# Forgetting attention begun by halves of the tokens, its value weights kept on chip, later sums in the post norms

## The chip, the cores and the metric

One core of a Trainium2 chip runs the whole program. Its engines work at the same time, each through an instruction queue of its own: TensorE (PE) multiplies, VectorE (DVE), ScalarE (ACT) and GpSimd (POOL) do elementwise work, and SyncE (SP) issues the transfers. The metric is the device time of one execution in microseconds (us), lower is better.

## What is computed

512 tokens of width 1024 go through two blocks. Block one is a mixer (gated linear attention, sliding-window attention and pooling, merged by gates, projected by `w_out`) and a conv-GeGLU feed-forward layer; both end in a norm of the result before it is added to x. Block two has forgetting attention ("fox"), a feed-forward layer, latent attention, another feed-forward layer and a last norm. The change touches the seam from the mixer's output to the first feed-forward layer, and the seam from there to fox:

```python
        x = x + rmsnorm(merged @ w_out[l], norm_mix_post[l])
        h = rmsnorm(x, norm_ffn_pre[l])
        f = conv_ffn(h, ffn_w_up[l], ffn_conv_w[l], ffn_conv_b[l], ffn_w_down[l])
        x = x + rmsnorm(f, norm_ffn_post[l])
...
    proj = h @ w_in
    qkv = proj[..., :3 * FOX_WIDTH].reshape(b, s_len, 3, FOX_HEADS, FOX_HEAD_DIM)
    q, k, v = qkv[:, :, 0], qkv[:, :, 1], qkv[:, :, 2]
    logf = jax.nn.log_sigmoid((proj[..., 3 * FOX_WIDTH:] + b_f).astype(jnp.float32))
    cum = jnp.cumsum(logf, axis=1)
```

## The kernel before

Activations lie with the channels on the partitions, x as eight tiles of 128 x 512 (tokens along the row). A product in fp32 accuracy is three matmuls: each operand is split into a rounded high part and a low rest, and high x high, high x low and low x high are added in PSUM. Weights come from memory in chunks of 128 x 1024 (512 KB, eight units of 128 x 128) in the order of a plan (`tfk_plan`). `_split` (lines 266 to 282) sends one chunk into a `raw` buffer (there are two), ScalarE casts it to `hi` (L277), VectorE subtracts to get `lo` (L278). The next-but-one transfer waits until both have read `raw`. `hi` and `lo` come from a pool of three buffers each; where `tfk_kept` holds for all units of a chunk (weights that are used twice) they are `khi` and `klo` in slots, large buffers shared with activations, and stay there until their second use.

A sublayer's end is `post_norm` (from L936). Its last projection tiles are done by halves of the tokens (256 each), so that the second half is computed while the first is finished. Each half's `chain(h)` is: sums of squares over the channels by TensorE (tile `tok`, two columns per half), a reciprocal square root in small steps on VectorE (`ra`, `ry`, `rh`, `rt`, L470 to L481), a diagonal matrix of it (`diag`, L490), which a matmul with ones spreads over all partitions (`bc`); then for each of eight tiles VectorE scales `yo` by `bc` (L962), GpSimd adds it to x (L963), and `x_ready` (L533) makes what the next sublayer needs: high part of x times the gain on ScalarE (`xs`, L420), low part on VectorE (`xs`, L421), squares on ScalarE (`sq`, L504), added up in `acc` by GpSimd, the eighth tile's by VectorE (L507). After the second half, one task (`stats`) takes the sums of all four token groups (`tok`, four columns), the square root, and `bc` of 512 columns, copied to `rsb`: the norm factor that the next sublayer multiplies into its results, not into its inputs, so its matmuls can begin before the factor is there.

The order of TensorE's work is written by the program: a clock counts the matmuls issued, and a task such as a chain's sums or its `bc` is put in when the clock has passed its due time, a number in `LAG`. The order on the other engines comes from a scheduler when the program is built, with no regard to the chip's real times: what stands in an engine's queue is done in that order, and an instruction whose input is late holds up all behind it.

Around the two places, in before: after `wout` come 288 matmuls of `up0` (six tiles, two halves of 256 tokens, 144 each, weights in `khi`, `klo`), whose results stay in PSUM until `rsb` is there. After `down0` comes `fox`: values for heads 0 to 7 of the first half (`fv`, 48 matmuls of 512 columns), the forget gates (`narrow`, 16), the first query tile (`fq`, 24), then the same for the second half with `fv`'s weights sent again, then the values of heads 8 to 15 for all tokens (96 matmuls), then keys (`fk`) and scores. Values are split into `fV` with the norm factor of their tokens.

## Time and profile before

| | |
|---|---|
| median of 3 runs (lowest, highest) | 2225.93 us (2223.95, 2228.35) |
| the profiled execution | 2225.05 us |
| its span in the profile | 2223.3 us |
| busy: PE, DVE, ACT, POOL | 97%, 64%, 46%, 13% |
| chain that ended last: PE, DVE, ACT, issue | 84%, 9%, 3%, 2% |
| chunk transfers (raw), median time to landing | 359 of 512 KB, 3.5 us |

The profile is one execution on the chip. A timeline row gives start and duration of an instruction, or of several alike in a row, and in brackets how long the engine stood idle before it and what ended that. Matmul durations overlap; the distance between starts is their pace. PEclk in the windows is the granted clock of TensorE as a share of full speed; 1.00 is 2.4 GHz, the lower of its two levels, 1.2 GHz, is 0.5.

### The profile page before, as it was taken

The page shows a single profiled execution, that of the slowest core. Times are in us where ns is not written, and L with a number is a line of the kernel's source. Part 1 is how long each engine was busy: PE and PEld are TensorE (multiplying, and loading weights), DVE is VectorE, ACT ScalarE, POOL GpSimd, SP SyncE. Part 2 cuts the span into 40 slices and gives each one's busy share as a digit, 9 for nine tenths or more (in the row PEclk, how much of TensorE's full clock was granted, in tenths as well). Part 3 has the DMA queues.
Part 4 walks back from the last instruction along what each step waited for, and adds up shares of the span by engine and source line. Part 5 has one row for each costly group of instructions (what it writes and reads, how often), then busy time and mean ns, then how long its engine had stood idle before and what let it go on. Part 6 is the DMA issues. An engine that isn't in the chain of part 4 may idle for free.

```text
span 2223.3 us, 27520 instructions
## 1 busy us (share of the span) xinstructions
PE 2165.1 (97%) x10536; PEld 1822.0 (82%) x10536; DVE 1423.7 (64%) x2372; ACT 1022.2 (46%) x1676; POOL 282.1 (13%) x242
## 2 busy tenths in 40 slices
PE   8989999999999998999999999999999999999998
PEld 6777788898888897888888888887888888888887
DVE  6897545578777238787677774357646567777524
ACT  4454232445444235676544443245755655444322
POOL 5221000040000004464200000102100101000010
PEclk9999999999999999999999999999999999999999
DMA  4211333322233344433233323332122223333332
GB/s 163 76 39 48 95 95 95 114 89 73 96 101 97 95 126 133 134 105 97 84 93 97 95 95 98 101 100 76 48 76 67 67 60 98 99 95 95 96 103 96
DMA packets 61956, 206.29 MB, mean 93 GB/s; under 512 B 7152, under 2 KB 9584, under 8 KB 61824
## 3 DMA queue, kind: packets, MB, share of 16 engines
q1 hardware_dynamic: 61392, 203.74, 29.4%
q8 instruction: 83, 1.36, 0.2%
q10 hardware_dynamic: 432, 0.79, 0.1%
q14 instruction: 49, 0.40, 0.1%
HBM read 197.65 MB, written 2.13 MB: 90 GB/s over the span
## 4 chain that ended last, share of the span: by engine, by line
PE 84%; DVE 9%; ACT 3%; issue 2%; DMA 1%; POOL 0%; SPq 0%; DVEq 0%; ACTq 0%; POOLq 0%
PE up L340 32%; PE down L340 15%; PE mout L340 4%; PE uq L340 3%; PE sc L340 2%; PE gate_a L340 2%; PE gate_b L340 2%; PE gate_c L340 2%; PE wout L340 2%; PE fout L340 2%; DVE lo L278 2%; DVE xs L421 1%; PE mpo L340 1%; PE dq L340 1%; PE fq L340 1%
## 5 line engine op out<-in xcount | busy, mean ns | idle before, releaser
L278 DVE TENSOR_TENSOR lo<-raw,hi 128x1024 fp32r<-128x1024 f32 (+1 forms) x348 | 438.1, 1259 | 318.0 <-ACT hi L277 313.6
L340 PE MATMUL up<-xs,hi 128*128 128x512 f32 x2016 | 621.8, 390 | 0.0
L277 ACT CAST hi<-raw 128x1024 fp32r<-128x1024 f32 (+1 forms) x348 | 365.2, 1049 | 554.2 <-PE down L340 170.5
L340 PEld LDWEIGHTS up<-xs,hi 128*128 128x128 f32 x2016 | 378.3, 188 | 78.9 <-issue 1.0
L340 PE MATMUL up<-xs,lo 128*128 128x512 f32 x1008 | 392.2, 389 | 0.0
L340 PE MATMUL down<-hl,hi 128*128 128x512 f32 (+1 forms) x1188 | 332.6, 366 | 0.0
L340 PEld LDWEIGHTS down<-hl,hi 128*128 128x128 f32 x1188 | 214.9, 189 | 36.2
L340 PEld LDWEIGHTS up<-xs,lo 128*128 128x128 f32 x1008 | 189.3, 188 | 39.6
L340 PE MATMUL down<-hl,lo 128*128 128x512 f32 (+1 forms) x594 | 217.1, 365 | 0.0
L507 POOL TENSOR_TENSOR acc<-acc,sq 128x256 f32<-128x256 f32 (+1 forms) x48 | 56.1, 1169 | 765.2 <-ACT sq L504 763.6
L1024 DVE TENSOR_TENSOR u<-up,rsb 128x512 f32<-128x512 f32 x132 | 90.1, 685 | 80.9 <-PE up L340 76.7
L1026 ACT ACTIVATE c<-u,par 128x512 f32<-128x512 f32 x132 | 107.0, 814 | 59.9 <-DVE u L1024 59.8
L340 PEld LDWEIGHTS down<-hl,lo 128*128 128x128 f32 x594 | 112.0, 189 | 18.0
L1027 DVE SCALAR_TENSOR_TENSOR c<-u,par,c 128x511 f32<-128x511 f32 x132 | 98.3, 746 | 23.8 <-ACT c L1026 23.7
L963 POOL TENSOR_TENSOR x<-x,yo 128x256 f32<-128x256 f32 x32 | 28.6, 930 | 633.3 <-DVE yo L962 633.3
L1028 DVE SCALAR_TENSOR_TENSOR c<-u,par,c 128x510 f32<-128x510 f32 x132 | 98.8, 749 | 4.0
L340 PE MATMUL uq<-hl,hi 128*128 128x512 f32 x288 | 89.5, 391 | 1.4 <-POOL hl L458 1.4
L457 ACT CAST hl<-c 128x512 fp32r<-128x512 f32 x66 | 40.7, 617 | 104.6 <-DVE c L1035 104.6
L340 PE MATMUL mout<-hl,hi 128*128 128x512 f32 x256 | 79.9, 393 | 0.0
L1033 ACT ACTIVATE c<-c 128x512 f32<-128x512 f32 x66 | 41.6, 630 | 70.4 <-DVE c L1028 70.3
L421 DVE SCALAR_TENSOR_TENSOR xs<-x,par,xs 128x512 fp32r<-128x512 f32 (+1 forms) x64 | 61.9, 1005 | 8.0 <-ACT xs L420 8.0
L340 PEld LDWEIGHTS uq<-hl,hi 128*128 128x128 f32 x288 | 53.9, 188 | 13.3 <-POOL hl L458 1.8
(398 smaller groups left out, 3933.9 us busy)
## 6 DMA issues: line engine op xcount, KB each, us to landing
raw<-in_wall_dram SPq DMA_DIRECT2D x359, 512.0 KB, 3.5
K<-KH SPq DMA_DIRECT2D x36, 128.0 KB, 2.3
bias<-cumd SPq DMA_DIRECT2D x16, 256.0 KB, 4.1
out_dram<-x SPq DMA_DIRECT2D x8, 256.0 KB, 2.3
x<-in_x_dram SPq DMA_DIRECT2D x7, 256.0 KB, 6.0
raw<-in_wall_dram SPq DMA_DIRECT2D x2, 256.0 KB, 3.9
early<-in_cst_dram SPq DMA_DIRECT2D x1, 512.0 KB, 6.5
msk<-in_msk_dram SPq DMA_DIRECT2D x1, 512.0 KB, 6.6
```

The source lines that it names most:

```text
L277: nc.scalar.copy(out=hi[:, c], in_=raw[:, c])
L278: nc.vector.tensor_tensor(out=lo[:, c], in0=raw[:, c], in1=hi[:, c].bitcast(F32), op=ALU.subtract)
L340: self.nc.tensor.matmul(out, lhsT=a, rhs=b, start=start, stop=stop)
L421: nc.vector.scalar_tensor_tensor(out=lo, in0=src, scalar=scale, in1=hi.bitcast(F32), op0=ALU.mult, op1=ALU.subtract)
L457: nc.scalar.copy(out=hi, in_=src)
L507: (eng or self.nc.vector).tensor_tensor(out=acc[:, cols], in0=acc[:, cols], in1=sq[:, cols], op=ALU.add)
L963: nc.gpsimd.tensor_tensor(out=x, in0=x, in1=yt, op=ALU.add)
L1024: v.tensor_tensor(out=u, in0=ps, in1=rsb, op=ALU.mult)
L1026: nc.scalar.activation(out=c, in_=u, func=AF.Identity, scale=self.p(conv, 88 + t), bias=self.p(conv, 132 + t))
L1027: v.scalar_tensor_tensor(out=c[:, 1:], in0=u[:, 0:T - 1], scalar=self.p(conv, 44 + t), in1=c[:, 1:], op0=ALU.mult, op1=ALU.add)
L1028: v.scalar_tensor_tensor(out=c[:, 2:], in0=u[:, 0:T - 2], scalar=self.p(conv, t), in1=c[:, 2:], op0=ALU.mult, op1=ALU.add)
L1033: nc.scalar.activation(out=g, in_=g, func=func)
```

## The change

1. The plan sends `fv`'s first half once (4 chunks fewer: 355 in the place of 359), in chunks of its own (`align`), and `tfk_kept` holds for `fv`, so all its chunks are `khi`, `klo` in slots.
2. The second chain's sums are due later: `keep_up` 6.5 after `wout`, `keep_fv` 9.0 after `down0`, in the place of 3.5.
3. The next sublayer's norm factor comes by halves (`half_stats_task`): two columns of sums, a root and a `bc` of 256 columns for each half.
4. `fox` does the values by halves: heads 0 to 7 and 8 to 15 of the first half, then both of the second.
5. Two masks (`lows`) move from a constant buffer into slots (39 in the place of 37), filled with zeros by GpSimd where they are needed.

```diff
@@ -112,6 +112,5 @@
     ffn(0)
+    align()
     cols("fv", 0, 8, 0, 4)
-    align()
     cols("fq", 0, 8, 0)
-    cols("fv", 0, 8, 0, 4)
     cols("fv", 0, 8, 4, 4)
@@ -158,3 +157,3 @@
     return e and (e[0] == "wout" and e[2] >= WOUT_WHOLE or e[0] == "up0" and (e[2] % DFF_T) * 2 < UP0_FIRST
-                  or e[0] == "fq" and e[2] == 0)
+                  or e[0] == "fq" and e[2] == 0 or e[0] == "fv")
 
@@ -167,3 +166,3 @@
 LAG = {
-    "sums_first": 19.0, "lat": 3.19, "lat_rsqrt": 5.85, "sums": 8.32, "sums_late": 13.0, "rsqrt": 6.9, "chain": 5.9, "keep": 3.5,
+    "sums_first": 19.0, "lat": 3.19, "lat_rsqrt": 5.85, "sums": 8.32, "sums_late": 13.0, "rsqrt": 6.9, "chain": 5.9, "keep": 3.5, "keep_up": 6.5, "keep_fv": 9.0,
     "last": 2.8, "last_rsqrt": 3.7,
@@ -205,3 +204,3 @@
         self.psum = ctx.enter_context(tc.tile_pool(name="psum", bufs=8, space=bass.MemoryType.PSUM))
-        self.nslot, self.nt2 = 37, 9
+        self.nslot, self.nt2 = 39, 9
         self.x = [self.slot([P, 2, T], F32, "x") for _ in range(4)]
@@ -214,3 +213,2 @@
         nc.gpsimd.memset(self.ones, 1.0)
-        self.lows = [self.cpool.tile([P, 2, T], F32R, name=f"lows{i}") for i in range(2)]
         self.ident = self.c("ident", 128)
@@ -432,2 +430,8 @@
 
+    def make_lows(self, n):
+        self.lows = [self.slot([P, 2, T], F32R, "lows") for _ in range(n)]
+        for a in self.lows:
+            for j in range(2):
+                self.nc.gpsimd.memset(a[64 - 64 * j:128 - 64 * j, j].bitcast(F32), 0.0)
+
     def stack_k(self, k):
@@ -525,2 +529,16 @@
 
+    def half_stats_task(self, acc, h):
+
+        pt = self.ps("tok")
+        self.tok_sums(acc, pt, (2 * h, 2 * h + 1))
+        rs = self.rsqrt(pt[:, 0:2], 1.0 / 1024, 2)
+        yield LAG["rsqrt"]
+        pb = self.bcast(rs)
+        if h == 0:
+            self.rsb = self.pool.tile([P, T], F32, tag="rsb", name="rsb", bufs=2)
+        self.nc.scalar.copy(out=self.rsb[:, HALVES[h]], in_=pb[:, 0:256])
+        self.rs_half[h].set(rs)
+        if h == 1:
+            self.rs.set((self.rsb, None))
+
     def x_start(self, nxt):
@@ -532,2 +550,3 @@
             self.xs = [Fut(self) for _ in range(8)]
+            self.rs, self.rs_half = Fut(self), [Fut(self) for _ in range(2)]
 
@@ -556,4 +575,6 @@
             nc.scalar.activation(out=x, in_=x, func=AF.Copy, scale=self.p("final", k))
-        elif k == 7 and cols != HALVES[0]:
-            self.rs = self.stats(self.acc, 1024, "sums_first" if self.next_gain == "mix_pre" else "sums" if cols == ALL else "sums_late")
+        elif k == 7 and cols == ALL:
+            self.rs = self.stats(self.acc, 1024, "sums_first" if self.next_gain == "mix_pre" else "sums")
+        elif k == 7:
+            self.tasks.insert(0, [self.half_stats_task(self.acc, HALVES.index(cols)), self.clock + LAG["sums_late"]])
 
@@ -597,5 +618,3 @@
         nc.gpsimd.memset(glow, 0.0)
-        for a in self.lows:
-            for j in range(2):
-                nc.gpsimd.memset(a[64 - 64 * j:128 - 64 * j, j].bitcast(F32), 0.0)
+        self.make_lows(1)
         v.tensor_tensor(out=glow[0:16], in0=self.add_narrow(pl, 32, 16), in1=rsb[0:16], op=ALU.mult)
@@ -683,3 +702,3 @@
                     ms.append(self.split_scaled(m, 0.5))
-        self.post_norm("wout", ms, "mix_post", nxt, WOUT_WHOLE, WOUT_WHOLE)
+        self.post_norm("wout", ms, "mix_post", nxt, WOUT_WHOLE, WOUT_WHOLE, "keep_up")
 
@@ -935,3 +954,3 @@
 
-    def post_norm(self, name, xs, gain, nxt, group, whole):
+    def post_norm(self, name, xs, gain, nxt, group, whole, late):
 
@@ -970,3 +989,3 @@
                 keep(t, self.proj(name, t, xs, 0, pss[t - whole], HALVES[h]), HALVES[h])
-            self.tasks.insert(0, [chain(h), self.clock + LAG["keep"]])
+            self.tasks.insert(0, [chain(h), self.clock + LAG[late if h else "keep"]])
 
@@ -1037,3 +1056,3 @@
         if post:
-            self.post_norm(f"down{i}", acts, post, nxt, 0, WHOLE[i])
+            self.post_norm(f"down{i}", acts, post, nxt, 0, WHOLE[i], "keep_fv")
         else:
@@ -1086,18 +1105,21 @@
         outs = [Fut(self) for _ in range(8)]
-        V = []
-
-        def values(pss):
-            rst = self.rs.get()[1]
-            for m, ps in enumerate(pss):
+        self.make_lows(2)
+        V = [None] * 8
+
+        def values(g, h):
+            pss = self.proj_tok("fv", 4 * g, self.halves[h], range(2 * h, 2 * h + 2))
+            rst = self.rs_half[h].get()
+            for i, ps in enumerate(pss):
                 vt = self.slot([P, 8, 2, 64], F32R, "fV")
-                self.split_scaled(ps.rearrange("p (h d) -> p h d", h=8), rst[:, m:m + 1], (vt[:, :, 0], vt[:, :, 1]))
-                V.append(vt)
-
-        pss, pf, pq = [], self.ps("narrow"), self.ps("fq")
+                self.split_scaled(ps.rearrange("p (h d) -> p h d", h=8), rst[:, i:i + 1], (vt[:, :, 0], vt[:, :, 1]))
+                V[4 * g + 2 * h + i] = vt
+
+        pf, pq = self.ps("narrow"), self.ps("fq")
         for h, cols in enumerate(HALVES):
-            pss += self.proj_tok("fv", 0, self.halves[h], range(2 * h, 2 * h + 2))
+            values(0, h)
             self.proj_narrow(fgt, self.halves[h], pf, cols)
             self.proj("fq", 0, self.halves[h], 0, pq, cols)
+            if h == 0:
+                values(1, h)
         rsb, _ = self.rs.get()
-        values(pss)
         z = self.t2([16, T], F32, "fz")
@@ -1112,3 +1134,3 @@
         nc.sync.dma_start(out=cumd, in_=cum)
-        values(self.proj_tok("fv", 4, xs))
+        values(1, 1)
         tri = self.c("swa", 256)[:, 128:256].unsqueeze(1).to_broadcast([P, 4, P])
```

**Place A, VectorE, after wout.** The rows run from the second chain's `diag` on. `yo` and `xs` are that chain's scaled outputs and the next sublayer's low inputs, `klo` and `lo` weight chunks of `up0`. Before:

```order
L490 TENSOR_TENSOR diag<-cst,ry 128x256
L278 TENSOR_TENSOR klo<-raw,khi 128x1024
L962 TENSOR_TENSOR yo<-yo,bc 128x256 x8
L278 TENSOR_TENSOR lo<-raw,hi 128x1024
L421 SCALAR_TENSOR_TENSOR xs<-x,par,xs 128x256 x2
L278 TENSOR_TENSOR lo<-raw,hi 128x1024
L421 SCALAR_TENSOR_TENSOR xs<-x,par,xs 128x256 x6
L278 TENSOR_TENSOR lo<-raw,hi 128x1024
```

After the change, from the last steps of the second chain's square root; the second `diag` is the factor of the first half:

```order
L484 SCALAR_TENSOR_TENSOR rt<-ry,rh 128x1 x2
L494 TENSOR_TENSOR diag<-cst,ry 128x256
L485 SCALAR_TENSOR_TENSOR ry<-rt,ry 128x2
L276 TENSOR_TENSOR lo<-raw,hi 128x1024
L981 TENSOR_TENSOR yo<-yo,bc 128x256 x8
L276 TENSOR_TENSOR lo<-raw,hi 128x1024
L419 SCALAR_TENSOR_TENSOR xs<-x,par,xs 128x256 x3
L276 TENSOR_TENSOR lo<-raw,hi 128x1024
L419 SCALAR_TENSOR_TENSOR xs<-x,par,xs 128x256 x2
L494 TENSOR_TENSOR diag<-cst,ry 128x256
```

The factor of the first half now has a `diag` of its own, behind the eight `yo` and five `xs` of the second chain; before, that factor came with the second half's, after all of them.

**Place A, TensorE, after wout.** The same two `diag` as TensorE uses them, in the middle of `up0`'s first 288 matmuls (the first `bc` stands after 111 of them, the sums of the chain and of the first half together after 63; before, the chain's sums stood after 33 and its `bc` after 84):

```order
L338 MATMUL bc<-diag,ones 128x256
L338 MATMUL up_3746<-xs,khi 128x256 x2
L338 MATMUL up_3746<-xs,klo 128x256
L338 MATMUL up_3747<-xs,khi 128x256 x2
L338 MATMUL up_3747<-xs,klo 128x256
L338 MATMUL up_3748<-xs,khi 128x256 x2
L338 MATMUL up_3748<-xs,klo 128x256
L338 MATMUL bc<-diag,ones 128x256
```

Nine matmuls stand between the second chain's `bc` and that of the first half's factor.

**Place B, VectorE, after down0.** The rows begin at the first chain's scaled outputs; `lo` are `fv`'s chunks. Before:

```order
L962 TENSOR_TENSOR yo<-yo,bc 128x256 x8
L278 TENSOR_TENSOR lo<-raw,hi 128x1024
L421 SCALAR_TENSOR_TENSOR xs<-x,par,xs 128x256 x4
L278 TENSOR_TENSOR lo<-raw,hi 128x1024
L421 SCALAR_TENSOR_TENSOR xs<-x,par,xs 128x256 x4
L507 TENSOR_TENSOR acc<-acc,sq 128x256
L470 TENSOR_SCALAR ra<-tok 128x2
```

After the change:

```order
L981 TENSOR_TENSOR yo<-yo,bc 128x256 x8
L419 SCALAR_TENSOR_TENSOR xs<-x,par,xs 128x256 x8
L511 TENSOR_TENSOR acc<-acc,sq 128x256
L276 TENSOR_TENSOR klo<-raw,khi 128x1024 x2
L511 TENSOR_TENSOR acc<-acc,sq 128x256
L304 TENSOR_TENSOR nhl<-nraw,nhl 128x8x32
L276 TENSOR_TENSOR klo<-raw,khi 128x1024 x4
L474 TENSOR_SCALAR ra<-tok 128x2
```

The two subtractions that stood ahead of and between the `xs` are now `klo` behind all eight; after two small ones four more follow, and only then `ra`, the root of the second chain, together with that of the first half, 21 steps up to these rows' `diag`:

```order
L485 SCALAR_TENSOR_TENSOR ry<-rt,ry 128x2 x2
L494 TENSOR_TENSOR diag<-cst,ry 128x256
L484 SCALAR_TENSOR_TENSOR rt<-ry,rh 128x1 x2
L419 SCALAR_TENSOR_TENSOR fV<-fv_6731,ry,fV 128x8x64
L485 SCALAR_TENSOR_TENSOR ry<-rt,ry 128x2
L419 SCALAR_TENSOR_TENSOR fV<-fv_6732,ry,fV 128x8x64
L494 TENSOR_TENSOR diag<-cst,ry 128x256
```

On TensorE the two `bc` of these `diag` stand after the first 48 `fv` matmuls and two `narrow` later; the sums stand after 39 and 42.

## Rows read from the trace of the kernel before

**Rows 1.** The page, part 1: busy time of each engine, its share, instructions
```profile
PE 2165.1 (97%) x10536; PEld 1822.0 (82%) x10536; DVE 1423.7 (64%) x2372; ACT 1022.2 (46%) x1676; POOL 282.1 (13%) x242
```

**Rows 2.** The waits of PE, whole run: in total us, times, longest us
```profile
PE tok L340 <- DVE acc L507: 7.9, 4, 4.7
...
PE fv L340 <- DVE xs L421: 1.3, 2, 0.7
...
PE fv L340 <- DVE lo L278: 1.0, 1, 1.0
```

**Rows 3.** Timelines of POOL and PE at the start: start us, duration us, engine, line
```profile
0.98 2.21 POOL L600 MEMSET lows<- 64x512 f32 x4
...
21.29 9.85 POOL L552 TENSOR_TENSOR acc<-acc,sq 128x512 f32<-128x512 f32 x5
...
33.35 0.95 PE L340 MATMUL tok<-ones,acc 128*128 128x1 f32 x8
```

**Rows 4.** Timeline of PE, 467 to 512 us
```profile
468.01 0.40 PE L340 MATMUL up<-xs,khi 128*128 128x256 f32 x2
...
474.70 0.79 PE L340 MATMUL tok<-ones,acc 128*128 128x1 f32 x4 [2.57 <-DVE acc L507]
...
506.13 1.02 PE L340 MATMUL bc<-diag,ones 128*128 128x512 f32 x2
```

**Rows 5.** Windows: stretch, length, busy us of each engine, granted clock (PEclk)
```profile
475.00:478.50 3.50, 3.50 (x18) 3.50 (x18) 2.79 (x12) 0.57 (x1) 0.00 (x0) 0.52 0.74 195
```

**Rows 6.** Timeline of DVE, 466 to 512 us
```profile
477.65 0.35 DVE L480 SCALAR_TENSOR_TENSOR rt<-ry,rh 128x1 f32<-128x1 f32 x2
479.01 1.23 DVE L278 TENSOR_TENSOR klo<-raw,khi 128x1024 fp32r<-128x1024 f32 x1 [1.00 <-ACT khi L277]
480.15 0.15 DVE L481 SCALAR_TENSOR_TENSOR ry<-rt,ry 128x2 f32<-128x2 f32 x1
480.34 0.42 DVE L490 TENSOR_TENSOR diag<-cst,ry 128x256 f32<-128x256 f32 x1
481.57 1.23 DVE L278 TENSOR_TENSOR klo<-raw,khi 128x1024 fp32r<-128x1024 f32 x1 [0.80 <-ACT khi L277]
483.51 2.74 DVE L962 TENSOR_TENSOR yo<-yo,bc 128x256 f32<-128x256 f32 x8 [0.72 <-PE bc L340]
486.17 1.77 DVE L278 TENSOR_TENSOR lo<-raw,hi 128x1024 fp32r<-128x1024 f32 x1
487.87 1.84 DVE L421 SCALAR_TENSOR_TENSOR xs<-x,par,xs 128x256 fp32r<-128x256 f32 x2
```

**Rows 7.** Timeline of ACT, 466 to 512 us
```profile
483.91 1.06 ACT L277 CAST hi<-raw 128x1024 fp32r<-128x1024 f32 x1 [2.38 <-DMA raw<-in_wall_dram]
```

**Rows 8.** Timeline of POOL, 466 to 512 us
```profile
484.01 7.96 POOL L963 TENSOR_TENSOR x<-x,yo 128x256 f32<-128x256 f32 x8 [10.79 <-DVE yo L962]
```

**Rows 9.** Timeline of PE, 836 to 910 us
```profile
838.91 0.40 PE L340 MATMUL fv<-hi,xs 128*128 128x512 f32 x1
...
848.83 1.01 PE L340 MATMUL tok<-ones,acc 128*128 128x1 f32 x4 [4.72 <-DVE acc L507]
...
859.03 1.99 PE L340 MATMUL narrow<-xs,nhl 128*64 128x256 f32 x16
...
863.73 0.40 PE L340 MATMUL fv<-hi,xs 128*128 128x512 f32 x1
...
884.01 0.79 PE L340 MATMUL fv<-hi,xs 128*128 128x512 f32 x1
...
906.22 0.62 PE L340 MATMUL fk<-xs,hi 128*128 128x512 f32 x2
```

**Rows 10.** Windows: the slow stretch after the wait in fv
```profile
849.70:854.00 4.30, 4.30 (x11) 3.39 (x12) 4.02 (x12) 0.00 (x0) 0.00 (x0) 0.52 0.28 107
```

**Rows 11.** Timeline of DVE, 836 to 888 us
```profile
837.43 1.83 DVE L278 TENSOR_TENSOR lo<-raw,hi 128x1024 fp32r<-128x1024 f32 x1
...
883.42 2.73 DVE L421 SCALAR_TENSOR_TENSOR fV<-fv,ry,fV 128x512 fp32r<-128x512 f32 x4
```

## The prediction

> **What bounds the kernel now.** I read the page's busy shares first [rows 1]: TensorE is busy for 97% of the span, all others for 64% or less. The change takes no matmul away (the products, sums and broadcasts have the same columns, cut otherwise), so it can only work through TensorE's waits. The table of TensorE's waits comes next [rows 2]: the sums of squares that wait for VectorE's last addition into acc cost 7.9 us, 4 times, the longest 4.7. The timeline shows two of these four where the change works: 2.57 us after the mixer's projection [rows 4] and 4.72 us in the first value projection [rows 9]. Both are followed by a stretch at a granted clock of 0.52, the lower level: 3.5 us of it [rows 5] and 4.3 us [rows 10]. At half speed that loses 3.5 x 0.48 = 1.7 us and 4.3 x 0.48 = 2.1 us. So the most that the later sums can win is 2.57 + 1.7 + 4.72 + 2.1 = 11.1 us. What a reader should look at next is VectorE, whose queue is fixed at build time: what stands there ahead of the small instruction (diag, the factor as a diagonal matrix) for which TensorE waits.
>
> **Edits with one answer.** Sending fv's first half once takes 4 transfers, 4 casts and 4 subtractions away: on engines that are not the bound, so 0; the other chunks keep their order on SP's queue. Place B shows where that cover ends. Two zero fills of the mixer's masks now stand on GpSimd between the additions for the first norm. One takes 2.21 / 4 = 0.55 us; the additions end at 31.14, TensorE sums at 33.35 [rows 3]; the 1.1 us fits into the 2.2 us between, so 0. The fox's four fills stand in GpSimd's idle time between the chains: 0.
>
> **Place A, wout to up0.** Today: up starts at 468.01, and 33 of its matmuls have gone when the wait for the sums begins at 474.70 - 2.57 = 472.13, so one every 0.12 us; bc of the whole factor is reached at 506.13, with 24 of the group's 288 matmuls left: 506.13 + 0.5 + 2.9 = 509.5 [rows 4]. After the change, step by step:
> - The second chain's sums go from matmul 33 to 63, together with the first half's. TensorE gets there at 468.01 + 63 x 0.12 = 475.6, some 0.4 later if it has to wait for a klo; the acc is done by 474.7. The 2.57 and the 1.7 are gone. With both pairs of sums (0.5) it goes on at 476.5.
> - bc of the chain stands at matmul 111: reached at 476.5 + 48 x 0.12 = 482.3. Its diag is now behind two klo and the steps of two interleaved square roots. The second klo ends at 482.80, since its chunk arrives no earlier [rows 6], and ten small instructions follow at 0.19 us (from one at 480.15 to the next at 480.34) and diag itself at 0.42 [rows 6]: ready at 485.1. **A wait of 2.8.**
> - bc of the first half's factor stands only 9 matmuls later, reached at 486.5. On VectorE its diag stands behind the eight yo, which need the bc just made, then two lo and five xs. The same work in the trace: yo takes 2.74, lo 1.77 beside GpSimd, two xs 1.84, so 0.92 each [rows 6]. From 486.1: 2.74 + 2 x 1.77 + 5 x 0.92 + 0.42 = 11.3, so 497.4. **A wait of 10.9.** Its bounds: none of it can start before the chain's bc, and GpSimd must first have added five of the eight x, about 1.0 each [rows 8], so not below 486.4 + 5 + 1.5 = 492.9, a wait of 6.4, if both lo were free; above, a late chunk for lo (the cast at 483.91 starts 3.7 us after the klo that freed its buffer ended at 480.24 [rows 6, 7]) adds up to 2.
> - Then 168 matmuls: 20.2, the slow clock after so long a gap 1.7 (the price of the 3.5 us stretch, the nearest row), sums and bc 0.8: 497.4 + 22.7 = 520.1. Against 509.5 that is +10.6; I take **+10.5**, bounds +6 and +13. Everything waits for this factor: all up results stay in PSUM until rsb is written, and TensorE's next group needs those banks.
>
> **Place B, down0 to the fox's keys.** Today fv starts at 838.91 and the keys follow at 906.22, 67.3 us [rows 9]. TensorE waits in it for 4.72, for xs and lo 2.3 [rows 2], and loses 2.1 to the clock. The rates: 96 fv matmuls take 906.22 - 884.01, so 0.231 each; narrow is 1.8 of the 4.7 us that narrow and fq take in a half, from 859.03 to 863.73 [rows 9]. After:
> - fv's chunks now lie in slots that ffn0's activations hold until down ends. The first chunk's klo therefore stands on VectorE behind all eight xs and an acc. VectorE is free for xs from 837.43 (a lo takes that place now [rows 11]); 8 x 0.92 = 7.4, acc like one more xs, 0.9, klo 1.7 beside GpSimd: 847.4. Today the first chunk's lo, a row at 837.43, ends as down does. **TensorE idles from 838.9 to 847.3** but for two matmuls, 7.9 us, in the place of today's 4.72 and the waits for xs. The slow clock behind it is 2.1 again.
> - 46 matmuls and two pairs of sums later, 847.3 + 10.6 + 2.1 + 0.7 = 860.7, bc of the chain: its diag stands behind four klo in a row and 21 small steps of two square roots. There are two raw buffers, so a chunk's cast starts 3.7 us after the klo before last ended; cast and subtraction take 1.06 and 1.23 [rows 6, 7], so the klo end at 853, 855, 859 and 861.2; 21 x 0.19 + 0.42 more: 865.6. **A wait of 4.9.**
> - bc of the half factor two narrow matmuls behind it: two fV at 0.68 [rows 11], three small steps and diag itself (1.0) follow the chain's diag: 868.0, **a wait of 2.0**, and 2 more at the slow clock.
> - Then narrow, fq (to 874.9) and 42 matmuls of the second group to 884.6; the second half's sums need the last acc, at about 885.6 after eight yo, GpSimd's eight x and six acc: **a wait of 1**. The rest, 54 matmuls, narrow, fq and 48 matmuls, is 12.5 + 4.7 + 11.1 + 0.7: keys at 914.6 instead of 906.2, **+8**. Bounds: 0, if the chunks arrive in less than 3.7 and the two bc waits vanish (6.9, with the clock's 2), and +13, if the longer of them doubles. The decay's biases follow narrow, which ends no later against the keys' end than today by more than their slack; I count 0.
>
> **Sum.** 10.5 + 8 = +18.5 against the profiled execution's 2225.05 (its span is 2223.3): 2243.6. The median of the three runs is 0.9 higher than that execution; I say **2244**. 0.2%, what a measurement of this kernel can tell from no change, is 4.5 us.
>
> **A rule beside a row.** While GpSimd adds x without a break from 484.01 on, about 1.0 each [rows 8], a lo takes 1.77 us, alone 1.23 [rows 6]: the two slow each other, but both go on. The Trainium skill, page "SBUF — State Buffer", section "Who interferes with whom", says that a VectorE instruction with two SBUF inputs and a GpSimd instruction that reads SBUF exclude each other, the later one blocking until the first has ended. The trace does not show that here.
>
> **The rivals.**
> - *The other side: the sums' waits go and nothing takes their place.* Time 2225.05 - 11.1 = 2214. It decides at two points: whether diag of the half factor can be ready by 486.5 in A, and the first klo by 838.9 in B. For it: the removed waits are real rows [rows 2]. Against it: VectorE works its queue in order (the small steps behind the klo at 479.01 started after it, though their input was done at 478.0 [rows 6]), so diag would have to be 11 us earlier and klo 8.5. 0.04.
> - *A loses, B wins its waits back.* If the slots come free earlier than I read and B runs with no wait, it gains today's 4.72 + 2.3 + 2.1 = 9.1 against A's 10.5: 2226, no change. 0.04.
> - *A alone.* B's waits only replace today's: 2235.5. For it: B's start loses 7.9 where 4.72 and part of the 2.3 go. Against: the two bc waits. 0.10.
> - *The engines exclude each other.* Then each of the two lo and five xs in A waits out one addition of 1.0 and gains at most 2 x 0.54 back: about 5.5 us later, 2249. By the rule named above this is the time; the row speaks against it. 0.04.
> - *Worse in B.* Each of the three new gaps there is followed by a slow stretch, and a late chunk moves the second half's chain too: +17 in B, 2253. 0.08.
> - The forecast, both places as worked out: 0.70.
>
> **How the numbers follow.** The forecast's own bounds are +6 + 0 and +13 + 13, 2231 to 2251; both low ends at once are unlikely. The range 2232 to 2252 takes in A alone and the excluding engines, and leaves out the first two rivals and most of the worse one, some 0.15. Faster by over 0.2%: 0.04. Within: 0.04. Slower: 0.92, all the others.
>
> **What would show it.** In A: no idle time before the sums, but bc waiting for diag twice, 2.8 and 10.9 us, the second behind xs on VectorE, and the granted clock at the lower level after it. In B: fv's first klo matmul near 847, bc waits of about 5 and 2, keys 75 to 76 us after down's end. Wrong if bc of the half factor waits under 3 us, or if VectorE's diag runs ahead of the xs; or if fv starts before 843, since then the slots were free earlier than I say; or if a wait that stands in neither place makes the time.

## The result, and the profile after

The changed kernel takes **2242.43 us** (median of four runs, 2241.65 to 2244.69) against 2225.22 us for the kernel before beside it: 1.0081 times as long, 95% interval 1.0065 to 1.0097 (the ratios here and below are those on record with each run, and need not equal the quotient of the two medians). One of the nine executions of e1 below, at 8255.47 us, lies far above all others and is left out of its median and ratio. The forecast was 2244 us, slower, with a range of 2232 to 2252.

The profiled execution after took 2244.69 us, its span is 2242.9 us. Four marks on TensorE cut both spans into the same stages: the first `up` matmul after `wout`, the first `up` that takes the whole `xs` (end of place A), the end of `down0`'s matmuls, the first `fk` (end of place B).

| stage (us) | before | after | difference |
|---|---|---|---|
| start to first `up` | 468.0 | 470.0 | +2.0 |
| place A: first `up` to first `up<-xs,hi` | 41.8 | 53.0 | **+11.2** |
| to the end of `down0` | 329.1 | 329.3 | +0.2 |
| place B: to first `fk` | 67.3 | 73.7 | **+6.4** |
| first `fk` to first `fout` | 130.3 | 131.2 | +0.9 |
| `fout` to the next block's `dkv` | 425.0 | 423.9 | -1.1 |

Busy time, from the page (as [rows 1]): TensorE works as long as before, 2167.1 us against 2165.1; the 19.6 us of span are idle time and slow clock.

```profile
PE 2167.1 (97%) x10540; PEld 1823.8 (81%) x10540; DVE 1418.9 (63%) x2394; ACT 1019.1 (45%) x1674; POOL 280.1 (12%) x244
```

The waits of TensorE after (total us, times, longest), answering to [rows 2]: of the sums' 7.9 us 1.3 are left, and a new row leads the table, the broadcast that waits for VectorE's `diag`.

```profile
PE bc L338 <- DVE diag L494: 19.2, 6, 11.4
```

Place A on TensorE after (timeline, start, duration; answers to [rows 4]): the eight sums no longer wait; the chain's `bc` waits 1.68, the half factor's 11.37.

```profile
470.01 0.40 PE L338 MATMUL up<-xs,khi 128*128 128x256 f32 x2
...
478.05 0.95 PE L338 MATMUL tok<-ones,acc 128*128 128x1 f32 x8
486.53 0.67 PE L338 MATMUL bc<-diag,ones 128*128 128x256 f32 x2 [1.68 <-DVE ry L485]
499.64 1.19 PE L338 MATMUL bc<-diag,ones 128*128 128x256 f32 x2 [11.37 <-DVE diag L494]
...
523.05 0.81 PE L338 MATMUL up<-xs,hi 128*128 128x512 f32 x2
```

The same stretch on VectorE (as [rows 6]): between the two `diag` stand the eight `yo`, three `lo` and five `xs`, one of those `lo` ahead of the `yo`.

```profile
485.97 0.42 DVE L494 TENSOR_TENSOR diag<-cst,ry 128x256 f32<-128x256 f32 x1
...
487.13 1.23 DVE L276 TENSOR_TENSOR lo<-raw,hi 128x1024 fp32r<-128x1024 f32 x1 [0.68 <-ACT hi L275]
488.27 2.73 DVE L981 TENSOR_TENSOR yo<-yo,bc 128x256 f32<-128x256 f32 x8
490.93 1.71 DVE L276 TENSOR_TENSOR lo<-raw,hi 128x1024 fp32r<-128x1024 f32 x1
492.56 2.68 DVE L419 SCALAR_TENSOR_TENSOR xs<-x,par,xs 128x256 fp32r<-128x256 f32 x3
495.16 1.75 DVE L276 TENSOR_TENSOR lo<-raw,hi 128x1024 fp32r<-128x1024 f32 x1
496.83 1.80 DVE L419 SCALAR_TENSOR_TENSOR xs<-x,par,xs 128x256 fp32r<-128x256 f32 x2
498.55 0.94 DVE L494 TENSOR_TENSOR diag<-cst,ry 128x256 f32<-128x256 f32 x1
```

Place B on TensorE (as [rows 9]): `fv` begins with two waits, and both `bc` and the second half's sums wait a little.

```profile
857.34 0.79 PE L338 MATMUL fv<-khi,xs 128*128 128x512 f32 x1 [4.83 <-ACT khi L275]
860.33 0.79 PE L338 MATMUL fv<-klo,xs 128*128 128x512 f32 x1 [2.20 <-DVE klo L276]
...
877.49 0.67 PE L338 MATMUL bc<-diag,ones 128*128 128x256 f32 x2 [2.57 <-DVE diag L494]
...
879.57 1.12 PE L338 MATMUL bc<-diag,ones 128*128 128x256 f32 x2 [1.17 <-DVE diag L494]
...
897.20 0.58 PE L338 MATMUL tok<-ones,acc 128*128 128x1 f32 x4 [1.29 <-DVE acc L511]
...
926.07 0.62 PE L338 MATMUL fk<-xs,hi 128*128 128x512 f32 x2
```

On VectorE (as [rows 11]) the first `klo` stands where the prediction put it, behind eight `xs` and an addition:

```profile
850.64 7.11 DVE L419 SCALAR_TENSOR_TENSOR xs<-x,par,xs 128x256 fp32r<-128x256 f32 x8
857.67 0.95 DVE L511 TENSOR_TENSOR acc<-acc,sq 128x256 f32<-128x256 f32 x1
858.54 3.41 DVE L276 TENSOR_TENSOR klo<-raw,khi 128x1024 fp32r<-128x1024 f32 x2
...
873.29 1.23 DVE L276 TENSOR_TENSOR klo<-raw,khi 128x1024 fp32r<-128x1024 f32 x1 [1.18 <-ACT khi L275]
...
876.93 0.42 DVE L494 TENSOR_TENSOR diag<-cst,ry 128x256 f32<-128x256 f32 x1
```

The clock behind the gaps (windows: stretch, length, busy us of five engines, PEclk, DMA share, GB/s), as [rows 5, 10]: 1.00 at the sums of A, where before had 0.52, but low behind the `bc` of A and behind both gaps of B.

```profile
476.00:479.00 3.00, 2.78 (x24) 2.61 (x23) 2.52 (x7) 0.00 (x0) 0.00 (x0) 1.00 0.44 131
...
499.60:505.00 5.40, 5.36 (x26) 5.21 (x27) 2.83 (x4) 0.37 (x1) 2.06 (x3) 0.57 0.04 15
860.30:865.00 4.70, 4.67 (x11) 3.70 (x12) 2.32 (x3) 1.04 (x1) 2.64 (x5) 0.50 0.69 173
877.50:884.00 6.50, 5.33 (x26) 4.68 (x27) 6.40 (x14) 3.72 (x7) 1.74 (x3) 0.74 0.34 88
```

The rows account for the two places. A: waits 1.68 + 11.37 in place of 2.57 are +10.5; the clock loses 5.4 x 0.43 = 2.3 in place of 1.7, +0.6; together 11.1 of the measured 11.2. B: waits 4.83 + 2.20 + 2.57 + 1.17 + 1.29 = 12.1 in place of 4.72 + 1.3 + 1.0 + 0.4 = 7.5 (the last a second wait for sums, at 876.05) are +4.6; the clock loses 4.7 x 0.50 + 6.5 x 0.26 = 4.0 in place of 2.1, +1.9; together 6.5 against 6.4 measured.

### The profile page after: what moved, and what is told of

The parts are those of the page before. It is cut to its first block, busy times and chain, and to the rows that moved or that the text cites. A ratio compares the mean times of both kernels' runs of the same rounds, so it can differ in the third digit from the quotient of the medians.

```text
span 2242.9 us, 27522 instructions
## 1 busy us (share of the span) xinstructions
PE 2167.1 (97%) x10540; PEld 1823.8 (81%) x10540; DVE 1418.9 (63%) x2394; ACT 1019.1 (45%) x1674; POOL 280.1 (12%) x244
## 4 chain that ended last, share of the span: by engine, by line
PE 84%; DVE 9%; ACT 3%; DMA 2%; issue 2%; POOL 0%; SPq 0%; DVEq 0%; ACTq 0%; POOLq 0%
PE up L338 32%; PE down L338 15%; PE mout L338 4%; PE uq L338 3%; PE sc L338 3%; PE gate_a L338 2%; PE gate_b L338 2%; PE gate_c L338 2%; PE wout L338 2%; DMA raw<-in_wall_dram 2%; PE fout L338 2%; DVE lo L276 1%; PE mpo L338 1%; PE dq L338 1%; PE fk L338 1%
## 5 line engine op out<-in xcount | busy, mean ns | idle before, releaser
L276 DVE TENSOR_TENSOR lo<-raw,hi 128x1024 fp32r<-128x1024 f32 (+1 forms) x336 | 422.2, 1256 | 315.7 <-ACT hi L275 313.0
L275 ACT CAST hi<-raw 128x1024 fp32r<-128x1024 f32 (+1 forms) x336 | 352.8, 1050 | 544.3 <-PE down L338 168.3
```

The costliest lines, as they stand in the source:

```text
L275: nc.scalar.copy(out=hi[:, c], in_=raw[:, c])
L276: nc.vector.tensor_tensor(out=lo[:, c], in0=raw[:, c], in1=hi[:, c].bitcast(F32), op=ALU.subtract)
```

## The experiments

**Theory**: the order of VectorE's queue makes the time; the half factor's `diag` behind `yo` and `xs` in A, the kept values' late `klo` in B. **Rivals**: A is long because of where the second chain now stands, or because of the extra small matmuls; B is long because of the halves, not of the keeping; or the later sums are what costs. All medians below stand against before in the same runs; stage lengths are from each kernel's profiled execution. e10 and e11 test a second theory, on what B's gains turn into.

| run | median | ratio to before (95%) | A | B | `fk` to `fout` |
|---|---|---|---|---|---|
| before | 2225.22 | 1 | 41.8 | 67.3 | 130.3 |
| after | 2242.43 | 1.0081 (1.0065 to 1.0097) | 53.0 | 73.7 | 131.2 |
| e1 | 2231.71 | 1.0038 (1.0028 to 1.0049) | 41.7 | 72.1 | 132.8 |
| e2 | 2229.9 | 1.0025 (1.0015 to 1.0036) | 42.9 | 70.5 | 132.4 |
| e3 | 2253.49 | 1.0130 (1.0115 to 1.0145) | 54.4 | 80.7 | 132.4 |
| e4 | 2244.23 | 1.0092 (1.0077 to 1.0107) | 52.9 | 69.7 | 135.3 |
| e5 | 2222.95 | 0.9997 (0.9988 to 1.0005) | 39.3 | 67.9 | 132.3 |
| e6 | 2227.92 | 1.0018 (1.0008 to 1.0027) | 39.3 | 67.1 | 136.5 |
| e7 | 2229.67 | 1.0023 (1.0013 to 1.0033) | 39.4 | 65.3 | 139.0 |
| e8 | 2234.09 | 1.0041 (1.0028 to 1.0055) | 41.1 | 73.3 | 132.6 |
| e9 | 2222.95 | 0.9990 (0.9982 to 0.9999) | 39.2 | 66.5 | 131.8 |
| e10 | 2238.31 | 1.0063 (1.0046 to 1.0080) | 39.6 | 67.6 | 144.0 |
| e11 | 2239.67 | 1.0065 (1.0053 to 1.0077) | 39.6 | 65.1 | 149.5 |

**e8: both `diag` together, nothing else moved.** The half factor's `diag` is made before the task yields; TensorE's order stays that of after, row for row. (`bcast` is cut for it into `diag_of`, which makes the `diag`, and `spread`, which multiplies it with ones.)

```diff
...
         rs = self.rsqrt(pt[:, 0:2], 1.0 / 1024, 2)
+        dn = self.diag_of(rs)
         yield LAG["rsqrt"]
-        pb = self.bcast(rs)
+        pb = self.spread(dn)
```

> The change, with one thing moved: DVE makes both diagonal spreads of a half's factor (chain and half factor) together, ahead of the first half's products yo and the operands xs, so that the half factor's bc on PE (whose own place in PE's order is not touched) no longer finds its diagonal behind them. Theory (the 11.4 us wait is DVE's row order): the wait before the second bc falls under 1.5 us, the slow clock after it goes, up<-xs may wait some 2 us for the second xs, place A (first up khi to first up of xs) 41.5 to 44.5 us in place of 53.1; place B stays at 72 to 75, because there its wait was 1.2 us; in all 2229 to 2234 us. Rival (the second chain's position or the additional matmuls on PE make A long, the wait only shows it): A stays at 50 or more and the time at 2239 to 2243.

VectorE in place A now (timeline):

```profile
481.86 0.76 DVE L498 TENSOR_TENSOR diag<-cst,ry 128x256 f32<-128x256 f32 x2
482.65 1.23 DVE L276 TENSOR_TENSOR lo<-raw,hi 128x1024 fp32r<-128x1024 f32 x1
483.80 2.73 DVE L991 TENSOR_TENSOR yo<-yo,bc 128x256 f32<-128x256 f32 x8
```

and TensorE: the second `bc` follows without a wait, a wait of 1.20 for `xs` is new, and the stage ends 41.1 us after its first `up`, which was at 465.95.

```profile
482.77 0.67 PE L338 MATMUL bc<-diag,ones 128*128 128x256 f32 x2 [2.01 <-DVE diag L498]
484.34 0.60 PE L338 MATMUL bc<-diag,ones 128*128 128x256 f32 x2
...
489.12 0.39 PE L338 MATMUL up<-xs,khi 128*128 128x256 f32 x1 [1.20 <-DVE xs L419]
...
507.06 0.81 PE L338 MATMUL up<-xs,hi 128*128 128x512 f32 x2
```

One instruction of 0.4 us, moved on VectorE alone, takes 11.9 us off A, with the same matmuls and the second chain where it was. The theory holds for A, both rivals fall. The granted clock from 486.5 to 505 is 1.00. The median fell by 8.3 to the upper edge of what was expected, less than the 11.9 of A: the stages come from single executions, and e8's (2229.1) is the shortest of its five, after's the longest of its four.

**e1: the half factor's broadcast later instead.** The root is handed to the values at once, the first half's `bc` comes 14 clock units later.

```diff
         rs = self.rsqrt(pt[:, 0:2], 1.0 / 1024, 2)
-        yield LAG["rsqrt"]
+        self.rs_half[h].set(rs)
+        yield LAG["rsqrt"] + (0.0 if h else 14.0)
         pb = self.bcast(rs)
...
-        self.rs_half[h].set(rs)
```

> The change with one edit: bc of the first half's factor is due 14 units of the program's clock later (TensorE reaches it after 240 matmuls of up0 or so, in the place of 120), and the root itself is handed to fox at once, so that fox's values don't wait for that bc. VectorE's queue after wout stays as it was. Theory (the bc that stands 9 matmuls behind the chain's bc waits for a diag behind yo and xs): the 11.4 us wait in place A and the slow clock behind it go, in place B the second bc's wait of 1.2; 2226 to 2230 us. Rival (the later sums themselves cost it, by moving the second chain): what is lost in A only moves to a later wait, 2238 us or more.

A is 41.7, in before 41.8: the other way to free TensorE of the same wait gives the same stage. It is 2 us slower in all than expected; one row in B says why:

```profile
882.54 0.98 PE L338 MATMUL tok<-ones,acc 128*128 128x1 f32 x4 [4.08 <-DVE acc L511]
```

The second half's sums, which waited 1.29 in after, come due before their `acc` when the 3.7 us of `bc` waits ahead of them shrink to 0.3.

**e2: before with the later sums alone.**

```diff
-    "rsqrt": 6.9, "chain": 5.9, "keep": 3.5,
+    "rsqrt": 6.9, "chain": 5.9, "keep": 3.5, "keep_up": 6.5, "keep_fv": 9.0,
...
-            self.tasks.insert(0, [chain(h), self.clock + LAG["keep"]])
+            self.tasks.insert(0, [chain(h), self.clock + LAG[late if h else "keep"]])
```

> The kernel before with part 2 of the change alone (keep_up 6.5, keep_fv 9.0). Theory (the later sums are not what costs): A wins the 2.57 us wait and the slow clock behind it and pays some 2 us at the chain's bc and at the stats' sums; B keeps a wait of 4 to 5 us, now for the third chunk's lo that stands behind eight xs; together 2221 to 2229 us. Rival (later sums cost it): 2233 us or more.

The waits for the sums are gone, and nothing is won: A 42.9 for 41.8, B 70.5 for 67.3. What was delayed is the second half's chain, and its operands are late instead (in A `xs` 2.88, in B the rows below).

```profile
849.61 0.50 PE L340 MATMUL fv<-lo,xs 128*128 128x512 f32 x1 [3.03 <-DVE lo L278]
...
864.26 0.79 PE L340 MATMUL fv<-hi,xs 128*128 128x512 f32 x1 [4.24 <-ACT xs L420]
```

The median, 2229.9, lies just above what was expected. So the 11.1 us that the rival on the other side hoped for aren't there even without the other parts.

**e3: after with both sums at 3.5 again.**

> The change without its part 2 (both numbers at 3.5 again). Theory: in A the sums wait 2.6 us again, and the first half's bc, some 34 matmuls behind the chain's, still waits about 9 to 10 us for a diag behind yo and xs; in B the start is the same (first klo behind eight xs, 7 us), the chain's bc waits less. 2238 to 2246 us. Rival (the later sums cost it): 2232 us or less.

Slower than after by 11, more than expected. A pays both waits, 2.57 and 10.82. In B the expectation missed a thing: with the chain's sums earlier, its `bc` stands at 873.59, and the half factor's `diag` falls behind `yo` and `xs` here as well.

```profile
873.59 0.59 PE L338 MATMUL bc<-diag,ones 128*128 128x256 f32 x2
...
887.95 1.22 PE L338 MATMUL bc<-diag,ones 128*128 128x256 f32 x2 [12.38 <-DVE diag L494]
```

The later sums cost some 5 us alone (e2), but save 11 beside the half factors.

**e4: the values' weights sent twice again, the rest as in after.**

```diff
-    align()
     cols("fv", 0, 8, 0, 4)
+    align()
     cols("fq", 0, 8, 0)
     cols("fv", 0, 8, 4, 4)
+    cols("fv", 0, 8, 0, 4)
+    cols("fv", 0, 8, 4, 4)
...
-                  or e[0] == "fq" and e[2] == 0 or e[0] == "fv")
+                  or e[0] == "fq" and e[2] == 0)
```

> The change without its part 1: fv's chunks are sent for each pass (fv twice over, 363 chunks) into the pool's hi and lo, the order of the work by halves stays. Theory (the slots hold the first klo back behind eight xs): in B fv starts right after down0 and the waits of 4.8 and 2.2 us at its start go; a wait of 4 to 5 us for the third chunk's lo stays, and both bc waits. B from fv's start to the keys 68 to 72 us in the place of 73.9, time 2237 to 2241 us; A unchanged. Rival (the order of the bc alone costs B): 2241 us or more and fv waits at its start as long as now.

B is 69.7, inside what was expected: `fv` starts at `down`'s end with no wait for weights, so the 7.0 us at the start of B came from the slots. The time did not follow and missed what was expected, by 3 us: `fk` to `fout` grows from 131.2 to 135.3, with a row that after lacks. The first scores wait for K:

```profile
935.51 0.30 PE L340 MATMUL sc<-K,Q 128*128 128x128 f32 x1 [1.99 <-DMA K<-KH]
```

The granted clock is 0.66 over the 4.5 us behind it, 1.5 us more. Why K is late is read below, at e10.

**e5: before, its sums after `wout` later by 1.7 units** (`keep_up` 5.2, `keep` at 3.5 elsewhere).

> The kernel before with one number: after wout the second chain's sums are due at 5.2 in the place of 3.5 (17 matmuls later; 6.5 in the change), down0 as before. Theory (a diag that stands ahead of the last klo costs nothing, and the wait for sums shrinks to under 1 us without a slow stretch): up0's first group takes 38.5 to 40 us in the place of 41.9, 2222 to 2223.5 us. Rival (each delay of the second chain comes back at its xs, as up's wait of 2.9 us for xs in the run with the late sums alone): 42 us or more, 2225 or more.

A falls to 39.3 as expected, with no wait at the sums or `bc` and 0.78 at `xs`: between too early (2.57 for `acc`) and too late (2.88 for `xs` in e2).

```profile
486.56 0.39 PE L340 MATMUL up<-xs,khi 128*128 128x256 f32 x1 [0.78 <-DVE xs L421]
```

In the whole time it can't be told from before.

**e6: the edits of e1 and e4 together, the factor after `wout` whole again, at 5.2.**

> The order by halves with fv's chunks sent for each pass (no slots), the half factor's root handed to fox at once and its bc 14 units later, whole factor (not by halves) after wout, its sums due at 5.2. Theory: place A as in the run with 5.2 on the kernel before, 38.5 to 40 us; place B without the wait for the first khi and klo, without the bc waits of 11, 5 and 2 us, but with one of about 4 us for the second half's sums (as in the run with the factor later); from fv's start to the keys 65 to 69 us, 2221 to 2229 us. Rival (B is bound by the chunks' arrival once they are sent four times): 70 us or more in B, 2230 or more.

Both places are at or under before's length, and the total is still 0.18% above: 6.1 us came back between `fk` and `fout`, where the scores wait 2.83 us for K.

**e7: as e6, with the second half's sums and factor 5 units later**, so that its sums don't wait for `acc`.

> As the run before it, and the second half's sums due 5 units later. Theory: the 4 us wait for the last acc goes; B 62 to 66 us, 2218 to 2226 us, a version that beats both kernels if the heads' part after it does not lengthen. Rival (the wait moves to the whole factor, which the decay and the queries need): no change against the run before it.

B is 65.3, shorter than in any run so far, and the time is above what was expected: the rival on the decay was right. `fz`, the gates times the norm factor, from which the decay is made, starts at 894.74, and SyncE issues the first two heads' biases at 911.76 and K at 913.57, so that all of them are under way together. The first scores wait:

```profile
921.03 0.45 PE L340 MATMUL sc<-K,Q 128*128 128x128 f32 x1 [5.33 <-DMA K<-KH]
```

since K is issued 10.3 us after the first `fk` (in before 7.0) and then takes three times its usual 2.3 us (transfers of e7, 900 to 925 us: count, size, median us from issue to landing):

```profile
bias<-cumd SPq DMA_DIRECT2D x4, 256.0 KB, 5.8
...
K<-KH SPq DMA_DIRECT2D x4, 128.0 KB, 6.9
```

**e9: e6 with the second column half of the values kept**, the gates of the second half ahead of its values, the `bc` of its half factor 2.4 units earlier. Against e6:

```diff
-    cols("fv", 0, 8, 4, 4)
...
-                  or e[0] == "fq" and e[2] == 0)
+                  or e[0] == "fq" and e[2] == 0 or e[0] == "fv" and e[2] >= 4)
...
-        yield LAG["rsqrt"] + (0.0 if h else 14.0)
+        yield LAG["rsqrt"] + (-2.4 if h else 14.0)
...
-            values(0, h)
+            if h == 0:
+                values(0, h)
             self.proj_narrow(fgt, self.halves[h], pf, cols)
             self.proj("fq", 0, self.halves[h], 0, pq, cols)
-            if h == 0:
-                values(1, h)
+            values(1 - h, h)
```

> e6 with three edits: the values' weights kept for the second column half alone, the second half's narrow products (they feed the decay) ahead of its values, and its half factor's root called 2.4 units earlier. Theory (what B saved in e6 came back as the scores' wait for K, because the decay chain behind narrow had not moved): A 39.4, B 65 to 67.5, fk to the attention's output 130 to 133 in place of 136.5, wait of the scores for K under 1 us, in all 2220 to 2224 us. Rival (the chain behind the whole factor, not narrow, sets K's arrival): the wait for K stays over 2 us, fk to output 135 or more, in all 2226 to 2230 us.

`fz` starts at 887.43, the biases leave at 904.67 and K at 911.65, when they have landed; the first scores don't wait. The same transfers in e9:

```profile
bias<-cumd SPq DMA_DIRECT2D x4, 256.0 KB, 3.6
...
K<-KH SPq DMA_DIRECT2D x4, 128.0 KB, 2.3
```

All stages came out as expected, and the kernel is the first whose interval lies under before's, by 0.1% (0.9982 to 0.9999). That is less than the bound of 0.2% set ahead, so it is a version not slower than before, no more; e5, with one number changed, can't be told from it.

**e10 and e11: e6 and e7 with the decay on another queue.** A second theory for the wait for K in e6 was that SyncE's queue stands still until `cum` is there, and what is behind it comes late.

```diff
-        nc.sync.dma_start(out=cumd, in_=cum)
+        nc.gpsimd.dma_start(out=cumd, in_=cum)
...
-            nc.sync.dma_start(out=t[:, 0], in_=cumd[h:h + 1].to_broadcast([P, T]))
+            nc.gpsimd.dma_start(out=t[:, 0], in_=cumd[h:h + 1].to_broadcast([P, T]))
```

> e6 with one thing changed: the decay's transfers (cumd to memory, and each head's bias back) are issued by GpSimd instead of SyncE; TensorE's order is the same. Theory (in e6 SyncE's queue stands still until cum is there, the weight chunks queued behind it come late, and the cast of K's high part stands behind such a chunk's cast on ScalarE): the first scores' wait for K falls from 2.8 to under 1 us, fk to the attention's output from 136.5 to 130 to 133, A 39.4, B 67 as before, in all 2220 to 2224 us. Rival (K is late because VectorE makes the decay ahead of the scaled keys, whichever queue carries it): the wait stays over 2 us, the time at 2226 to 2229. A second rival: GpSimd's own work (the low parts of Q, the masked biases) comes late behind its transfers, a new wait of the scores for Q or bias, 2228 or more.

> e7 with the same edit. Theory: the scores' wait for K, 5.3 in e7 (its transfers took 6.9 us behind the biases' on SyncE's queue), falls under 2 us; what VectorE's own order costs (the scaled keys come behind the decay) may stay. B 65.3, fk to the attention's output 131 to 134, in all 2219 to 2224 us. Rival (the transfers share the same 16 engines, so another queue changes nothing): the wait stays over 4 us, the time at 2228 to 2231.

Both missed, by 14 us and more, on the slow side. The first wait for K shrinks only from 2.83 to 1.89 in e10 and from 5.33 to 3.87 in e11, and later heads wait as well: e6 waits for K twice, 4.7 us in all, e10 five times, 12.3 us, the longest this one.

```profile
991.58 0.30 PE L340 MATMUL sc<-K,Q 128*128 128x128 f32 x1 [3.95 <-DMA K<-KH]
```

That K took 5.4 us (median of its four transfers, 972 to 1000 us) with two biases and a chunk of weights beside it, and 2.3 in e6, where SyncE issued it ahead of the next two biases. The Trainium skill (page "DMA: Bandwidth & Descriptors", section "Issuing engines are not separate DMA queues") says that transfers run on the same 16 DMA engines and interleave, whichever engine started them; here the trace agrees, with 5.4 us against 2.3.

One step of the theory was right all the same. In e6 the cast of K's high part (`KH`, at 914.63) stands on ScalarE behind the cast of a chunk that came late:

```profile
913.68 1.05 ACT L277 CAST hi<-raw 128x1024 fp32r<-128x1024 f32 x1 [4.67 <-DMA raw<-in_wall_dram]
```

SyncE had issued that chunk at 908.26, right behind the first two biases and 0.9 us after VectorE's `lo` had freed its buffer (at 907.37), and it took 5.3 us beside the biases, where 3.5 is the median of the chunks. In e4 the same rows stand in the same order: a wait of 4.53 for a chunk that took 5.3, then `KH`. In e10 the chunk was issued as its buffer came free and took 3.5, and K was issued 9.9 us after the first `fk`, in e6 12.6 after it. What that won was lost again on the transfers: K beside the biases, 4.0 us at the first head and 5.4 later. So one queue's order is of use, for it keeps the biases out of K's way. One more thing changed with the queue and is not tried by itself: the profile counts GpSimd's transfers as another kind (software_dynamic), and `cumd` took 2.0 us in the place of 1.6.

## Why the prediction was right

- **Place A** (+10.5 forecast, +11.2 measured). Each step stands in the rows. The sums don't wait. The chain's `bc` waits 1.68 where 2.8 was said: `diag` was ready 16.4 us after the first `up` instead of 17.1, since small steps of two roots overlap and cost less than the 0.19 us taken from a dependent pair. The half factor's `bc` waits 11.37 (10.9 said): from the first `yo` to the end of `diag` it is 11.2 us where 11.3 was reckoned, but the `yo` begin 1.7 us after the chain's `bc` and not 1.0, behind a third `lo` that the sum left out. The clock behind it cost 2.3 (1.7 said). e8 and e1 show the cause by two separate ways.
- **Place B** (+8 forecast, +6.4 measured). The start: 7.0 us of waiting where 7.9 was said, and e4 shows that it is the slots. The chain's `bc` is the term that was mis-sized: 2.57 instead of 4.9. Counted from `fv`'s first `klo` matmul, TensorE got there 1.2 us later than reckoned, and `diag` was ready 1.3 us earlier: VectorE needed 2.9 us from the first small step at 874.43 to the end of `diag`, where 21 x 0.19 + 0.42 = 4.4 was counted, the same error as in A. The half factor's `bc` (1.17 for 2.0) and the second half's sums (1.29 for 1) came as said. That the decay costs nothing was right with little to spare: in after the first scores have no wait for K, in e4 1.99 us.
- **The total** is nearer than its terms deserve: A +0.7, B -1.6, +0.2 between them, +0.9 and -1.1 behind, and +2.0 from the start of the program, which the prediction did not have and which is no effect of the change (last section).
- **The rivals.** The other side (2214) falls by the rows, and e2 and e3 show that the waits removed come back even alone. A alone and worse in B are out by B's +6.4. The engines that exclude each other: the time that this rival gave is out, but not the rule behind it.

The prediction read from [rows 6] and [rows 8] that VectorE and GpSimd only slow each other. Its 1.0 us is a mean over eight additions of different lengths, and single instructions of before show something else:

```profile
486.11 0.75 POOL L963 TENSOR_TENSOR x<-x,yo 128x256 f32<-128x256 f32 x1
486.17 1.77 DVE L278 TENSOR_TENSOR lo<-raw,hi 128x1024 fp32r<-128x1024 f32 x1
486.80 1.73 POOL L963 TENSOR_TENSOR x<-x,yo 128x256 f32<-128x256 f32 x1
```

The addition that was first ends at 486.86, in no more time than the others beside `yo`; `lo` ends 1.08 us after it, the next addition 0.59 after `lo`. The other `lo` and `klo` that meet additions of this size keep the same distances (medians in both kernels: 1.08 us over 9 and 7 of them, 0.59 over 6 and 5). So each waits until the other has ended. The Trainium skill, page "SBUF — State Buffer", section "Who interferes with whom", says that a VectorE instruction with two SBUF inputs contends with a GpSimd instruction that reads SBUF, and that their shared ports are locked for one of them at a time; the trace agrees, with these distances. The rival's 5.5 us were wrong for another reason: the 1.77 of a `lo` and the 0.92 of an `xs`, taken from rows with the additions beside them, already contain these waits. Where the prediction took a row without them it was short: the `diag` of the half factor took 0.94 us, not 0.42, and ended 0.28 after an addition.

## What to carry to other kernels

When a task's sums are moved, ask for every small instruction behind them where it stands in its own engine's queue: a `diag` of 0.4 us cost 11.4 us on TensorE because eight `yo`, three `lo` and five `xs` stood ahead of it, and making it at the root, before the task yields, removed that wait. A wait for sums that is only pushed back returns at the operands of the same chain; there is a best place between, and it is found from the two waits (2.57 at one end, 2.88 at the other, 0.78 at 5.2). And a stage made shorter is not a kernel made shorter until the next thing that waits has been looked at: in three runs B's gain came back as a wait for K, in e4 and e6 because K's cast stood behind a chunk that had met the decay's transfers, in e7 because the factor put off was also the decay's, whose transfers then met K's.

## What the runs showed that was not expected

A transfer's time depended more on what was under way with it than on the queue that issued it: K's transfers of 128 KB took 2.3 us by themselves, and medians of 4.0 to 6.9 beside the biases of two heads (e7, e10, e11), from one queue or from two. A chunk of weights was under way there as well; no run has K beside the biases alone.

The same wait is not always followed by the slow clock. Some 77 us into both programs, where the change does nothing, TensorE stands idle for 2.31 us. In before it goes on at full speed, two `sk` matmuls in 0.70 us:

```profile
77.31 0.63 PE L345 MATMUL svt<-cst,sv 128*128 128x128 f32 x4 [2.31 <-issue]
77.69 0.70 PE L340 MATMUL sk<-xs,hi 128*128 128x512 f32 x2
```

In after the two take 1.20, the lower level:

```profile
77.68 1.09 PE L343 MATMUL svt<-cst,sv 128*128 128x128 f32 x4 [2.31 <-issue]
78.42 1.20 PE L338 MATMUL sk<-xs,hi 128*128 128x512 f32 x2
```

From 77 to 90 us the granted clock was 1.00 in before and 0.87 in after, which is 1.7 us of the 2.0 that the start cost. The first `up` came between 465.95 (e8) and 470.0 us (after, e3) in the profiled executions, in no relation to the edits; so a difference of 4 us between two profiled executions may lie ahead of the first edit, and stages are compared from their own first matmul. What decides whether the clock falls after such a wait stays open; no run here tries it.
